# Expert results copied out of PSUM by ScalarE, low parts on VectorE alone, the residual summed by TensorE in the last norm

## The chip, the cores and the metric

The kernel runs on one core of a Trainium2 chip. Its engines are called as in the profile: PE is TensorE, ACT ScalarE, DVE VectorE, POOL GpSimd, SP SyncE; PSUM is the memory that PE writes, SBUF the one in which tiles are kept. The metric is the time of one execution on the device in microseconds (us), the median of several runs.

## What is computed

One layer of an encoder on 1024 tokens of 1024 channels (h), all in float32. A token mixer (attention, convolution, Fourier) comes first; the change doesn't touch it. Then follows the mixture of experts and the last norm:

```python
h = layer_norm(x, ln_in_g, ln_in_b)
mix = token_mixer(h, ...)
h = layer_norm(DEEPNORM_ALPHA * h + mix, ln1_g, ln1_b)
# hier_moe: 4 groups of 8 experts; each token takes the best group and the two best experts in it
for g in range(N_EXPERT_GROUPS):
    a = einsum('nd,edf->nef', xt, w_gate[g])       # d = 1024, f = 256
    u = einsum('nd,edf->nef', xt, w_up[g])
    hid = silu(a) * u * combine[:, g, :, None]
    out = out + einsum('nef,efd->nd', hid, w_down[g])
h = layer_norm(DEEPNORM_ALPHA * h + out, ln2_g, ln2_b)
```

## The kernel before

The tokens of each expert are gathered into a block of up to 128 rows; there are 33 blocks, the 32 experts (b = 0 to 31) and one for rows that overflow an expert's 128. All 33 are unrolled in one loop (L1341). Float32 products are made of three matmuls on parts rounded to another format (`mm3`, L161 to L163): high by high, high by low, low by high. So each operand is split into a high part, a copy with rounding, and a low part, the difference.

A block's weights are six tiles of 128x1024 (512 KB each): four of gate and up (g0 to g3), two of down (dL, dH). SP loads them (`fetch`, L1212) into a ring of 22 raw tiles, in the order of the list `units`; `load_next` issues the next one, and it waits until the raw tile that it overwrites has been split. For each block

- POOL gathers the rows from h in DRAM (`gather`, L1215), three blocks ahead; PE transposes them (`xtr`, L1277), ACT and DVE split them (L1280, L1283);
- ACT makes the high part of each weight tile (`high`, L1251), DVE the low part (`low`, L1255), but for g1, whose low part POOL makes in two halves of 128x512, each with a dependency written by hand (`with_start_of`) that places it beside a certain DVE low part;
- PE runs the gate and up products (`gu`), ACT the silu (L1287), DVE `hidden` (L1291), PE transposes (`htr`, L1297), ACT and DVE split the result (`hT`, L1302, L1303), and PE runs the down products (`dn`);
- DVE combines (L1315): the gathered rows times a kept scale z per row, plus `dn` from PSUM, written over the gathered rows. POOL scatters that tile (L1318) to y in DRAM, which has two rows for a token, one of each of its experts. The residual alpha·h goes into y in this way.

The work of neighbouring blocks is interleaved as the loop is written: in one turn stand the low parts and down weights of block b-1, the gate and up products of b, and the splits of b+1. Every engine's order is the order in which the code issues, in this part on SP and POOL too. One step of the overflow's bookkeeping (L1133 to L1195) is issued on DVE in each turn until it is finished. `GA` = 6 buffers hold gathered rows; ACT fills each with zeros once (L1242).

Then comes a loop over further overflow blocks (L1403), which this input doesn't enter; a barrier of all engines stands there. The last norm (L1433 to L1447) takes 8 tiles of 128 tokens: SP loads y0 and y1 (L1436, L1437), DVE adds them and takes the row sum (L1439), then the mean (L1440); ACT squares into PSUM with a sum (L1442) and takes the root (L1443); DVE takes the reciprocal (L1444), and centres, scales and shifts in two steps (L1445, L1446), and SP stores (L1447).

## Time and profile before

| | us |
|---|---|
| median of 3 runs | 992.27 (991.0 to 992.88) |
| profiled execution, its own time | 985.81 |
| its span | 984.0 |
| PE busy in the span | 892.0 (91%) |
| DVE busy | 739.7 (75%) |
| POOL busy | 506.5 (51%) |
| ACT busy | 478.4 (49%) |
| first and last silu of the 33 blocks, start | 616.3, 929.3 |
| last combine, start | 939.54 |
| first load of the last norm, issue | 944.26 |

So the span has three parts that matter here: what stands ahead of the first expert block (616 us, its last piece the routing of the last token tile), the blocks (some 313 us), and the last norm (some 40 us). The shares of busy time are means over all three, so each part is read by itself, in windows. The times of single instructions come from this one execution, which took some 6 us less than the timed runs.

### The profile page before, as it was taken

The page shows a single profiled execution, that of the slowest core. Times are in us where ns is not written, and L with a number is a line of the kernel's source. Part 1 is how long each engine was busy: PE and PEld are TensorE (multiplying, and loading weights), DVE is VectorE, ACT ScalarE, POOL GpSimd, SP SyncE. Part 2 cuts the span into 40 slices and gives each one's busy share as a digit, 9 for nine tenths or more (in the row PEclk, how much of TensorE's full clock was granted, in tenths as well). Part 3 has the DMA queues.
Part 4 walks back from the last instruction along what each step waited for, and adds up shares of the span by engine and source line. Part 5 has one row for each costly group of instructions (what it writes and reads, how often), then busy time and mean ns, then how long its engine had stood idle before and what let it go on. Part 6 is the DMA issues. An engine that isn't in the chain of part 4 may idle for free. (4 is left out here: it accounts for less than half of the span.)

```text
span 984.0 us, 11512 instructions
## 1 busy us (share of the span) xinstructions
PE 892.0 (91%) x4059; PEld 655.5 (67%) x4059; DVE 739.7 (75%) x869; ACT 478.4 (49%) x591; POOL 506.5 (51%) x286
## 2 busy tenths in 40 slices
PE   8899999999999999999999765999999999999910
PEld 5788688878865555565468654767878777878710
DVE  7643993665555767758745864999999999999848
ACT  6442331142035344344524151867777777777623
POOL 0299910350065756656645203467677888776300
PEclk9999999999999999999999885999999999999955
DMA  7043111236311000080033334899999999999167
GB/s 299 22 141 135 54 43 65 73 102 227 130 49 51 1 1 1 1 305 22 24 129 125 134 128 148 283 321 341 387 386 388 381 355 356 366 363 373 74 226 298
DMA packets 57659, 179.74 MB, mean 183 GB/s; under 512 B 10816, under 2 KB 12224, under 8 KB 57600
## 3 DMA queue, kind: packets, MB, share of 16 engines
q1 hardware_dynamic: 46800, 158.43, 43.9%
q0 software_dynamic: 9504, 16.80, 4.6%
q10 hardware_dynamic: 1296, 3.76, 1.1%
q8 instruction: 32, 0.52, 0.2%
q14 instruction: 27, 0.22, 0.1%
HBM read 162.70 MB, written 34.08 MB: 200 GB/s over the span
## 5 line engine op out<-in xcount | busy, mean ns | idle before, releaser
L685 POOL TENSOR_TENSOR ssum<-ssum,p 128x1024 f32<-128x1024 f32 x48 | 117.3, 2444 | 33.6 <-ACT p L679 29.1
L1255 POOL TENSOR_TENSOR g1l<-raw,g1h 128x512 fp32r<-128x512 f32 x66 | 87.5, 1327 | 77.2 <-DVE g2l L1255 28.1
L679 ACT ACTIVATE p<-sc 128x1024 f32<-128x1024 f32 x64 | 65.6, 1025 | 97.9 <-PE sc L163 80.1
L653 DVE TENSOR_REDUCE mx<-mp 128x1 f32<-128x1024 f32 x64 | 77.2, 1218 | 30.1 <-PE mp L652 29.8
L1318 POOL DMA_INDIRECT y_d<-gx,wql x32 | 84.3, 2635 | 25.4 <-DVE gx L1315 25.1
L161 PE MATMUL ip<-hh,wh 128*128 128x512 f32 (+1 forms) x224 | 89.5, 401 | 0.0
L162 PE MATMUL ip<-hl,wh 128*128 128x512 f32 (+1 forms) x224 | 88.8, 396 | 0.0
L163 PE MATMUL ip<-hh,wl 128*128 128x512 f32 (+1 forms) x224 | 88.4, 395 | 0.0
L1215 POOL DMA_INDIRECT gx<-h_d,wql x32 | 56.0, 1750 | 55.7 <-DVE wql L1024 50.6
L692 PE MATMUL pv<-p,v 128*64 128x512 f32 x256 | 68.0, 614 | 0.0
L1255 DVE TENSOR_TENSOR g0l<-raw,g0h 128x1024 fp32r<-128x1024 f32 x33 | 54.2, 1643 | 0.0
L1251 ACT ACTIVATE g1h<-raw 128x1024 fp32r<-128x1024 f32 x33 | 35.0, 1061 | 30.2 <-PE gu L163 21.4
L163 PEld LDWEIGHTS ip<-hh,wl 128*128 128x128 f32 (+1 forms) x224 | 41.2, 184 | 10.2 <-DVE wl L215 0.3
L162 PEld LDWEIGHTS ip<-hl,wh 128*128 128x128 f32 (+1 forms) x224 | 41.3, 184 | 9.8 <-issue 0.7
L161 PEld LDWEIGHTS ip<-hh,wh 128*128 128x128 f32 (+1 forms) x224 | 41.3, 184 | 9.7 <-issue 0.5
L1315 DVE SCALAR_TENSOR_TENSOR gx<-gx,wql,dn 128x1024 f32<-128x1024 f32 x32 | 40.7, 1272 | 2.9 <-PE dn L163 2.9
L1255 DVE TENSOR_TENSOR g3l<-raw,g3h 128x1024 fp32r<-128x1024 f32 x33 | 41.0, 1242 | 0.0
L1277 PE MATMUL xtr<-ident,gx 128*128 128x128 f32 x264 | 35.1, 277 | 6.4 <-DMA gx<-h_d,wql 6.4
L703 DVE RECIPROCAL rec<-rec 128x256 f32<-128x256 f32 x16 | 26.9, 1724 | 18.3 <-ACT rec L701 18.3
L1255 DVE TENSOR_TENSOR g2l<-raw,g2h 128x1024 fp32r<-128x1024 f32 x33 | 40.0, 1212 | 0.9 <-ACT g2h L1251 0.5
L1255 DVE TENSOR_TENSOR dL<-raw,dL 128x1024 fp32r<-128x1024 f32 x33 | 40.1, 1214 | 0.0
L1255 DVE TENSOR_TENSOR dH<-raw,dH 128x1024 fp32r<-128x1024 f32 x33 | 40.0, 1213 | 0.0
(391 smaller groups left out, 2553.2 us busy)
## 6 DMA issues: line engine op xcount, KB each, us to landing
raw<-wgu SPq DMA_DIRECT2D x128, 512.0 KB
raw<-wd SPq DMA_DIRECT2D x63, 512.0 KB
fy<-y_d SPq DMA_DIRECT2D x16, 512.0 KB
wr<-wt SPq DMA_DIRECT2D x13, 512.0 KB
xt<-x SPq DMA_DIRECT2D x8, 512.0 KB
ah_d<-al SPq DMA_DIRECT2D x8, 512.0 KB
aq<-ah_d SPq DMA_DIRECT2D x8, 512.0 KB
pa_d<-aq SPq DMA_DIRECT2D x8, 512.0 KB
```

The costliest lines, as they stand in the source:

```text
L161: T.matmul(out, lh, rh, start=start, stop=False)
L162: T.matmul(out, lh, rl, start=False, stop=False)
L163: T.matmul(out, ll, rh, start=False, stop=stop)
L653: V.tensor_reduce(mxs[h][:, t:t + 1], ps, AX.X, ALU.max)
L679: S.activation(p, ps, AF.Exp)
L685: G.tensor_tensor(ssums[h], ssums[h], p, ALU.add)
L692: T.matmul(pvs[h][64 * i:64 * i + 64], vv[t // 2][:, t % 2, 64 * h:64 * h + 64], p[:, half(i)], start=t == 0, stop=t == NT - 1)
L1215: G.indirect_dma_start(out=g, out_offset=None, in_=h1_d, in_offset=bass.IndirectOffsetOnAxis(ap=idx, axis=0), bounds_check=NTOK - 1, oob_i ...
L1255: return eng.tensor_tensor(l[:, cs], where[b, j][:, cs], f32(h[:, cs]), ALU.subtract)
L1277: T.transpose(ps[:, tok(k)], g[:, tok(k)], ident)
L1315: V.scalar_tensor_tensor(g, g, z, DN.pop(b), op0=ALU.mult, op1=ALU.add)
L1318: return G.indirect_dma_start(out=y_d, out_offset=bass.IndirectOffsetOnAxis(ap=idx, axis=0), in_=g, in_offset=None, bounds_check=2 * NTOK ...
```

## The change

1. **Results.** DVE's combine is gone. ACT copies `dn` from PSUM into one of two new tiles `yo` (L1322 of the new file), and POOL scatters that. The scales z are no longer computed. y now holds expert results alone, without the residual. `GA` falls from 6 to 4 gathered tiles.
2. **Low parts.** All of them are made by DVE, g1's as one of 128x1024; POOL keeps gathers and scatters alone. In DVE's order g3's low part now stands ahead of `hT`, and g1's behind those of the down weights. The list `units` is put in the order in which the tiles are now split.
3. **Residual.** Eight loads of h (512 KB each) stand behind the last weights, in raw tiles that have been used. In the last norm PE adds by float32 matmuls into PSUM (`fin`): alpha times the identity (`alid`) by h, the identity by y1, and for the tiles t = 1, 3, 5 (`PESUM`) by y0 too. For these three ACT copies `fin` to SBUF with the row sum; for the other five DVE adds y0 to `fin`. y1 is loaded before y0. The square goes to SBUF (over y1), not to PSUM. The rows of scale and shift (g2, b2) are loaded earlier, when the bookkeeping's tiles are free.

```diff
-GA = 6
+GA = 4
+PESUM = (1, 3, 5)
...
-    units, taken = [(0, j) for j in (0, 2, 1, 3)], [0]
+    units, taken = [(0, j) for j in range(3)], [0]
     for b in range(NS + 1):
+        units += [(b, 3)] if b < NS else []
         units += [(b - 1, 4), (b - 1, 5)] if b > 0 else []
-        units += [(b + 1, j) for j in (0, 2, 1, 3)] if b + 1 < NS else []
+        units += [(b + 1, j) for j in (1, 0, 2)] if b + 1 < NS else []
+    units += [(NS, t) for t in range(NT)]
...
+    alid = kept_w[:, 0:P]
+    S.activation(alid, ident, AF.Copy, scale=ALPHA)
     gx = [big("M", f"gx{i}") for i in range(GA)]
+    yo = [big("M", f"yo{i}") for i in range(2)]
...
-    def combine(b, g, z):
-        V.scalar_tensor_tensor(g, g, z, DN.pop(b), op0=ALU.mult, op1=ALU.add)
+    def combine(b):
+        S.activation(yo[0 if b == "ov" else b % 2], DN.pop(b), AF.Copy)
...
-            if b < NS:
-                with_start_of(low(b, 1, G, half(1)), prev)
-                load_next()
             if b > 1:
-                o, g = b - 2, gx[(b - 2) % GA]
-                combine(o, g, stat[o][3])
-                st = scatter(g, stat[o][1])
+                combine(b - 2)
+                st = scatter(yo[b % 2], stat[b - 2][1])
...
             if b + 1 < NS:
                 high(b + 1, 1)
+                low(b + 1, 1)
+                load_next()
                 xtrans(b + 1, gx[(b + 1) % GA])
-                with_start_of(low(b + 1, 1, G, half(0)), prev)
...
     for t in range(NT):
-        y0, y1, r = big("H", "fy0"), big("H", "fy1"), big("O", "fr")
+        y0, y1, r, ps = big("H", "fy0"), big("H", "fy1"), big("O", "fr"), acc("fin")
+        nc.sync.dma_start(y1, y_d[tok(NT + t)])
         nc.sync.dma_start(y0, y_d[tok(t)])
-        nc.sync.dma_start(y1, y_d[tok(NT + t)])
         sc = sp.tile([P, 4], F32, name="sc", bufs=4)
-        V.scalar_tensor_tensor(r, y0, 1.0, y1, op0=ALU.mult, op1=ALU.add, accum_out=sc[:, 0:1])
+        terms = [(alid, where[NS, t]), (ident, y1)] + ([(ident, y0)] if t in PESUM else [])
+        for n, (m, v) in enumerate(terms):
+            for i in range(2):
+                T.matmul(ps[:, half(i)], m, v[:, half(i)], start=n == 0, stop=n == len(terms) - 1)
+        if t in PESUM:
+            S.activation(r, ps, AF.Copy, accum_out=sc[:, 0:1])
+        else:
+            V.scalar_tensor_tensor(r, ps, 1.0, y0, op0=ALU.mult, op1=ALU.add, accum_out=sc[:, 0:1])
         V.tensor_scalar(sc[:, 1:2], sc[:, 0:1], -1.0 / D, None, op0=ALU.mult)
-        junk = acc("junk")
-        S.activation(junk, r, AF.Square, bias=sc[:, 1:2], accum_out=sc[:, 2:3])
+        S.activation(y1, r, AF.Square, bias=sc[:, 1:2], accum_out=sc[:, 2:3])
```

Lines of the new file stand one lower from L36 on, and further off behind the deleted ones, so the orders below are matched by what they do.

**ACT ahead of the blocks, around the last token tile.** `xT` is the copy of its transposed rows that the routing's matmuls read, `rs` a root in its norm, gx the zero fills. Before:

```order
L933 ACTIVATE rs<-mv,eps 128x1
L1242 ACTIVATE gx_4024<-eps 128x1024
L1242 ACTIVATE gx_4025<-eps 128x1024
L1242 ACTIVATE gx_4026<-eps 128x1024
L1242 ACTIVATE gx_4027<-eps 128x1024
L954 ACTIVATE xT<-xtr 128x512
L1242 ACTIVATE gx_4028<-eps 128x1024
L1242 ACTIVATE gx_4029<-eps 128x1024
L1035 ACT_TABLE_LOAD
```

and now:

```order
L1243 ACTIVATE wql<-ident 128x128
L934 ACTIVATE rs<-mv,eps 128x1
L955 ACTIVATE xT<-xtr 128x512
L1249 ACTIVATE gx_4024<-eps 128x1024
L1249 ACTIVATE gx_4025<-eps 128x1024
L1249 ACTIVATE gx_4026<-eps 128x1024
L1249 ACTIVATE gx_4027<-eps 128x1024
L1032 ACT_TABLE_LOAD
```

The last `xT` stood behind four of the six zero fills; now it stands ahead of all four, and `alid` is new.

**DVE in one late block**, from the low part of g2 to the next block's. Before:

```order
L1255 TENSOR_TENSOR g2l<-raw_4011,g2h 128x1024
L1315 SCALAR_TENSOR_TENSOR gx_4029<-gx_4029,wql,dn 128x1024
L1303 TENSOR_TENSOR hT<-htr,hT 128x256
L1255 TENSOR_TENSOR g3l<-raw_4013,g3h 128x1024
L1255 TENSOR_TENSOR dL<-raw_4014,dL 128x1024
L1255 TENSOR_TENSOR dH<-raw_4015,dH 128x1024
L1283 TENSOR_TENSOR x0l<-xtr,x0h 128x1024
L1255 TENSOR_TENSOR g0l<-raw_4016,g0h 128x1024
L1291 SCALAR_TENSOR_TENSOR sh<-gu,wql,sh 128x256
L1255 TENSOR_TENSOR g2l<-raw_4017,g2h 128x1024
```

and now:

```order
L1262 TENSOR_TENSOR g2l<-raw_4005,g2h 128x1024
L1262 TENSOR_TENSOR g3l<-raw_4006,g3h 128x1024
L1310 TENSOR_TENSOR hT<-htr,hT 128x256
L1262 TENSOR_TENSOR dL<-raw_4007,dL 128x1024
L1262 TENSOR_TENSOR dH<-raw_4008,dH 128x1024
L1262 TENSOR_TENSOR g1l<-raw_4009,g1h 128x1024
L1290 TENSOR_TENSOR x1l<-xtr,x1h 128x1024
L1262 TENSOR_TENSOR g0l<-raw_4010,g0h 128x1024
L1298 SCALAR_TENSOR_TENSOR sh<-gu,wql,sh 128x256
L1262 TENSOR_TENSOR g2l<-raw_4011,g2h 128x1024
```

The combine is gone, g1's low part has come in behind dH's, and g3's stands ahead of `hT`.

**ACT in the same place**, from one silu to the next. Before:

```order
L1287 ACTIVATE sh<-gu 128x256
L1251 ACTIVATE g2h<-raw_4007 128x1024
L1251 ACTIVATE g3h<-raw_4009 128x1024
L1302 ACTIVATE hT<-htr 128x256
L1251 ACTIVATE dL<-raw_4010 128x1024
L1251 ACTIVATE dH<-raw_4011 128x1024
L1251 ACTIVATE g1h<-raw_4014 128x1024
L1280 ACTIVATE x0h<-xtr 128x1024
L1251 ACTIVATE g0h<-raw_4012 128x1024
```

and now:

```order
L1294 ACTIVATE sh<-gu 128x256
L1258 ACTIVATE g2h<-raw_4001 128x1024
L1258 ACTIVATE g3h<-raw_4002 128x1024
L1322 ACTIVATE yo_4028<-dn 128x1024
L1309 ACTIVATE hT<-htr 128x256
L1258 ACTIVATE dL<-raw_4003 128x1024
L1258 ACTIVATE dH<-raw_4004 128x1024
L1258 ACTIVATE g1h<-raw_4005 128x1024
L1287 ACTIVATE x1h<-xtr 128x1024
L1258 ACTIVATE g0h<-raw_4006 128x1024
```

The copy of `dn` into `yo` stands between g3's high part and `hT`; the rest is as it was.

**PE behind the last block**, where before it had nothing: `raw` are the tiles of h, `wql` holds `alid`, the odd and even `fy` are y1 and y0.

```order
L1443 MATMUL fin<-raw_4001,wql 128x512 x2
L1443 MATMUL fin<-raw_4002,wql 128x512 x2
L1443 MATMUL fin<-raw_4003,wql 128x512 x2
L1443 MATMUL fin<-fy_7055,ident 128x512 x2
L1443 MATMUL fin<-fy_7074,ident 128x512 x2
L1443 MATMUL fin<-fy_7073,ident 128x512 x2
L1443 MATMUL fin<-fy_7095,ident 128x512 x2
L1443 MATMUL fin<-raw_4004,wql 128x512 x2
L1443 MATMUL fin<-fy_7114,ident 128x512 x2
L1443 MATMUL fin<-fy_7113,ident 128x512 x2
L1443 MATMUL fin<-raw_4005,wql 128x512 x2
L1443 MATMUL fin<-fy_7135,ident 128x512 x2
```

The sums of h for three tiles come first, then y1 and y0 as the tiles go on; seven such lines of two matmuls follow, 19 in all.

## Rows read from the trace of the kernel before

**Rows 1.** Windows: us, busy time of each engine, granted clock, DMA share, GB/s.
```profile
720.00:740.00 20.00, 20.00 (x97) 16.12 (x96) 20.00 (x23) 15.85 (x20) 14.20 (x9) 1.00 1.02 398
860.00:880.00 20.00, 19.57 (x98) 15.79 (x97) 20.00 (x22) 15.25 (x19) 14.39 (x9) 1.00 0.98 365
900.00:920.00 20.00, 20.00 (x99) 16.53 (x98) 19.18 (x20) 16.16 (x20) 11.80 (x8) 1.00 0.71 272
```

**Rows 2.** Line L1287: count, durations in ns (min/median/max), first and last start.
```profile
L1287 ACT ACTIVATE sh<-gu x33: 384/385/387, 616.3 to 929.3; 128x256 f32<-128x256 f32 x33
```

**Rows 3.** Timeline, DVE, one late block: start, duration, instruction.
```profile
904.79 1.28 DVE L1315 SCALAR_TENSOR_TENSOR gx<-gx,wql,dn 128x1024 f32<-128x1024 f32 x1 [0.21 <-PE dn L163]
905.99 0.42 DVE L1303 TENSOR_TENSOR hT<-htr,hT 128x256 fp32r<-128x256 f32 x1
906.32 1.22 DVE L1255 TENSOR_TENSOR g3l<-raw,g3h 128x1024 fp32r<-128x1024 f32 x1
907.45 1.22 DVE L1255 TENSOR_TENSOR dL<-raw,dL 128x1024 fp32r<-128x1024 f32 x1
...
911.06 1.27 DVE L1255 TENSOR_TENSOR g0l<-raw,g0h 128x1024 fp32r<-128x1024 f32 x1
```

**Rows 4.** Timeline, DVE and POOL, a block of the slower stretch.
```profile
783.74 2.26 DVE L1255 TENSOR_TENSOR g0l<-raw,g0h 128x1024 fp32r<-128x1024 f32 x1
...
783.61 1.30 POOL L1255 TENSOR_TENSOR g1l<-raw,g1h 128x512 fp32r<-128x512 f32 x1
...
789.34 4.34 POOL L1318 DMA_INDIRECT y_d<-gx,wql  x1 [0.31 <-DVE gx L1315]
```

**Rows 5.** Timeline, ACT, late blocks; in brackets the idle time before and its releaser.
```profile
901.98 0.39 ACT L1287 ACTIVATE sh<-gu 128x256 f32<-128x256 f32 x1 [0.55 <-PE gu L163]
...
905.00 0.39 ACT L1302 ACTIVATE hT<-htr 128x256 fp32r<-128x256 f32 x1 [0.74 <-PE htr L1297]
...
907.91 1.06 ACT L1251 ACTIVATE g1h<-raw 128x1024 fp32r<-128x1024 f32 x1 [0.62 <-DMA raw<-wd]
...
911.38 0.39 ACT L1287 ACTIVATE sh<-gu 128x256 f32<-128x256 f32 x1 [0.55 <-PE gu L163]
```

**Rows 6.** SP waits in 700:780, then in 860:905: total, times, longest.
```profile
SPq L1212 <- DVE g0l L1255: 16.0, 8, 2.4
...
SPq L1212 <- DMA raw<-wgu: 21.5, 16, 2.4
```

**Rows 7.** Timeline around the last token tile (ACT, PE, DVE), then a group of the page.
```profile
581.18 3.87 ACT L1242 ACTIVATE gx<-eps 128x1024 f32<-128x1024 f32 x4
...
585.59 1.92 PE L961 MATMUL lg<-wql,xT 128*128 128x36 f32 x8 [4.20 <-ACT xT L954]
...
587.55 0.26 DVE L966 SCALAR_TENSOR_TENSOR lg<-lg,rs,base 128x36 f32<-128x36 f32 x1 [3.60 <-PE lg L961]
...
L1215 POOL DMA_INDIRECT gx<-h_d,wql x32 | 56.0, 1750 | 55.7 <-DVE wql L1024 50.6
```

**Rows 8.** Timeline of the end: last combine, first y load, first and last DVE steps.
```profile
939.54 1.28 DVE L1315 SCALAR_TENSOR_TENSOR gx<-gx,czo,dn 128x1024 f32<-128x1024 f32 x1 [3.50 <-PE dn L163]
...
944.26 0.34 SPq L1436 DMA_DIRECT2D fy<-y_d  x1
...
949.29 1.23 DVE L1439 SCALAR_TENSOR_TENSOR fr<-fy,fy 128x1024 f32<-128x1024 f32 x1 [8.47 <-DMA fy<-y_d]
...
979.10 1.29 DVE L1446 SCALAR_TENSOR_TENSOR fr<-fr,sc,b 128x1024 f32<-128x1024 f32 x1
```

**Rows 9.** Groups of the last norm, 943.6:984: busy us, mean ns.
```profile
L1442 ACT ACTIVATE junk<-fr,sc 128x1024 f32<-128x1024 f32 x8 | 8.9, 1116 | 27.5 <-DVE sc L1440 27.5
L1446 DVE SCALAR_TENSOR_TENSOR fr<-fr,sc,b 128x1024 f32<-128x1024 f32 x8 | 10.2, 1278 | 0.0
```

**Rows 10.** Timeline, PE, fp32 matmuls of 128x512 (six records), and the window after the barrier.
```profile
572.18 2.75 PE L1327 MATMUL warm<-ones 128*128 128x512 f32 x6
...
944.00:950.00 6.00, 0.00 (x0) 0.00 (x0) 0.71 (x1) 0.00 (x0) 0.00 (x0) 0.50 0.76 249
```

More of the change, by code (lines that the diff above doesn't have):

```diff
@@ L1024, in table @@
                 self.last = V.scalar_tensor_tensor(idx.rearrange("p j e -> p (j e)"), ps, EMPTY, tabs, op0=ALU.add, op1=ALU.add)
-    def keep_scale(out, ix):
-        V.tensor_tensor(out, ix[:, 1], ix[:, 0], ALU.subtract)
-        V.tensor_scalar(out, out, -ALPHA / NTOK, ALPHA, op0=ALU.mult, op1=ALU.add)
     def combine_weights():
@@ L1234, in load_next @@
             b, j = units[taken[0]]
-            fetch(where[b, j], j, source[b], eng or nc.sync)
+            if b == NS:
+                (eng or nc.sync).dma_start(where[b, j], h1_d[tok(j)])
+            else:
+                fetch(where[b, j], j, source[b], eng or nc.sync)
             taken[0] += 1
+    alid = kept_w[:, 0:P]
+    S.activation(alid, ident, AF.Copy, scale=ALPHA)
     gx = [big("M", f"gx{i}") for i in range(GA)]
+    yo = [big("M", f"yo{i}") for i in range(2)]
     for n in range(NRAW - 7):
@@ L1329, in build @@
             high(0, j)
-            if j in (0, 2):
-                prev = low(0, j)
+            if j < 3:
+                low(0, j)
         for n in range(3):
             load_next(nc.scalar)
-        low(0, 1, G, half(0))
         next(weigh)
@@ L1359, in build @@
             if 0 < b <= NS:
+                hsplit(b - 1)
                 for j in (4, 5):
                     high(b - 1, j)
-                    prev = low(b - 1, j)
+                    low(b - 1, j)
                     load_next()
@@ L1386, in build @@
                 high(b + 1, 2)
-                prev = low(b + 1, 2)
+                low(b + 1, 2)
                 load_next()
@@ L1395, in build @@
                 source[NE] = dynamic_src(ereg)
+                g2, b2 = late_rows
+                nc.sync.dma_start(g2, A["rows"][4:5].to_broadcast([P, D]))
+                nc.sync.dma_start(b2, A["rows"][5:6].to_broadcast([P, D]))
             if b < NS:
@@ L1398, in build @@
     assert spill is None and taken[0] == len(units)
-    g2, b2 = big("L", "g2"), big("L", "b2")
-    nc.sync.dma_start(g2, A["rows"][4:5].to_broadcast([P, D]))
-    nc.sync.dma_start(b2, A["rows"][5:6].to_broadcast([P, D]))
     n_ov = nc.values_load(nov[0:1, 0:1], min_val=0, max_val=NOV)
@@ L1407, in build @@
             fetch(where["ov", j], j, dynamic_src(e), nc.sync)
[L1408 removed]
+        ci, cf = sp.tile([P, 2], I32, name="ci"), sp.tile([P, 1], F32, name="cf")
         for j in range(2):
             V.tensor_copy(ci[:, j:j + 1], idxo[:, j, bass.ds(i, 1)])
[L1411 to L1412 removed]
+        V.tensor_copy(cf, cwo[:, bass.ds(i, 1)])
         gather(gx[0], ci[:, 0:1])
@@ L1421, in build @@
         silu("ov")
-        hidden("ov", cf[:, 0:1])
+        hidden("ov", cf)
         htrans("ov")
@@ L1429, in build @@
                 emm(ps[:, half(i2)], (hT[:, 0:256], hT[:, 256:512]), part(0, 4 + k), tok(k), half(i2), k == 0, k == 1)
-        combine("ov", gx[0], cf[:, 1:2])
-        scatter(gx[0], ci[:, 1:2])
+        combine("ov")
+        scatter(yo[0], ci[:, 1:2])
     for t in range(NT):
-        y0, y1, r = big("H", "fy0"), big("H", "fy1"), big("O", "fr")
+        y0, y1, r, ps = big("H", "fy0"), big("H", "fy1"), big("O", "fr"), acc("fin")
+        nc.sync.dma_start(y1, y_d[tok(NT + t)])
         nc.sync.dma_start(y0, y_d[tok(t)])
-        nc.sync.dma_start(y1, y_d[tok(NT + t)])
         sc = sp.tile([P, 4], F32, name="sc", bufs=4)
-        V.scalar_tensor_tensor(r, y0, 1.0, y1, op0=ALU.mult, op1=ALU.add, accum_out=sc[:, 0:1])
+        terms = [(alid, where[NS, t]), (ident, y1)] + ([(ident, y0)] if t in PESUM else [])
[4 more added lines that the diff above has]
+            S.activation(r, ps, AF.Copy, accum_out=sc[:, 0:1])
+        else:
+            V.scalar_tensor_tensor(r, ps, 1.0, y0, op0=ALU.mult, op1=ALU.add, accum_out=sc[:, 0:1])
         V.tensor_scalar(sc[:, 1:2], sc[:, 0:1], -1.0 / D, None, op0=ALU.mult)
-        junk = acc("junk")
-        S.activation(junk, r, AF.Square, bias=sc[:, 1:2], accum_out=sc[:, 2:3])
+        S.activation(y1, r, AF.Square, bias=sc[:, 1:2], accum_out=sc[:, 2:3])
         S.activation(sc[:, 3:4], sc[:, 2:3], AF.Sqrt, bias=eps[:, 0:1], scale=1.0 / D)
```

20 lines of the change are left out of this document (8 added, 12 removed).

## The prediction

> **What bounds the kernel now.** I read the windows first, then single engines inside a block, then the two ends. The 33 silu instructions start from 616.3 to 929.3 [rows 2]: 32 intervals in 313.0 us, 9.78 each. Near the end one interval takes 9.40 (901.98 to 911.38), and there ACT's idle time ends on PE at both silus' side and at `hT` [rows 5]; PE is busy 20.00 of 20 us in that window while DVE has 0.8 to spare [rows 1]. So 9.40 is what PE needs for a block, and 32 x 9.40 = 300.8 would be the loop at PE's pace. The other 12.2 us are lost elsewhere. Where? In the window from 720 on DVE is busy 20.00 of 20 [rows 1]: it has no slack at all, so whatever stretches an instruction of it stretches the block. And something does: g0's low part takes 1.27 in a late block [rows 3] and 2.26 at 783.74, where POOL's half of g1's low part begins at 783.61 and runs beside it [rows 4]. That POOL instruction stands behind a scatter of 4.34 [rows 4], which is why it comes at that moment; g0's low part takes over 2 us in nine blocks. SP, up to there, waits for DVE's low parts to free raw tiles, and only later for loads to land [rows 6]. So in the blocks DVE, with POOL's collisions, is the bound, and PE is close behind it.
>
> Two more pieces count. Ahead of the blocks POOL waits for the index table (50.6 us in all, the first gather) [rows 7], and in the routing that leads to it ACT does four zero fills from 581.18 for 3.87 us before it copies the last `xT`; PE idles 4.20 for that copy and DVE 3.60 for PE [rows 7]. At the end, from the first y load (944.26) to the end of DVE's last step (979.10 + 1.29 = 980.39), 36.1 us pass, and DVE sets that pace once the first pair has landed at 949.29 [rows 8].
>
> **The change, part by part.** I take each against the profiled span of 984.0.
>
> *The start.* `xT` no longer stands behind the zero fills. PE's rows have been ready since 581.4 (585.59 less 4.20), DVE's since 583.95 (587.55 less 3.60) [rows 7]. With `xT` at 581.4, 0.57 or so long, and the eight small matmuls at 1.92 at most [rows 7], the logits are there at about 583.9, when DVE is. That brings 3.6 us, and the chain to the gathers moves as a whole. The fills now stand behind, before the table load of the combine weights; they may hold that side chain up by about 1 us, which no gather waits for. Bounds: 0 (if something else, such as the transposes at the clock PE then has, were late next) to 3.6. I take 3.6, since both idle times end on this one copy.
>
> *The blocks.* DVE loses the combine (1.20 from start to start) and gains g1's low part, 1.13 by the spacing of g3 and dL [rows 3]: by itself nearly nothing. What counts is that POOL does no subtraction any more, so no collision is left: g0's low part goes from up to 2.26 back to about 1.2 [rows 3, 4]. Seven low parts at 1.13, `hT` at 0.33 (905.99 to 906.32) and 0.4 for `hidden` (estimate from its size and `hT`) make 8.65 per block, against PE's 9.40. The overflow's steps (up to 1 us in some early blocks, estimate) fit in the difference. So DVE stops being the bound, and PE becomes it: 12.2 us gained if every interval falls to 9.40. What remains of the old loss is at least 0; the ends of this term are -4 (only the nine blocks lose their collision of about 1.0, and half of that comes back as other waits) and -14 (the first and last interval lack a part and could be below 9.40). I take -12.2.
>
> *What hides the copy on ACT.* It is about as long as g1's high part, 1.06 [rows 5], some 0.95 from start to start. `dn` ends when the combine starts, 904.79 [rows 3]; `hT` began at 905.00 after 0.74 of idle [rows 5]. So the copy fills 0.2 of that idle and pushes `hT`, dL and dH back by 0.7. Behind them stood 0.62 of idle before g1's high part, and 0.55 before the next silu [rows 5]: the push of 0.7 is taken up by these two, 1.17. PE takes `hT` and the down weights only behind the next silu, about 5 us later. In DVE's queue g1's low part then waits for its high part, and `hidden`, behind it, comes some 0.2 later than now, with about 0.8 in hand before PE transposes. Cost: 0 by this reading; it is the thinnest margin of the change, and a rival below. `yo` has two tiles, so the copy waits for a scatter of two blocks earlier, 18.8 us against 4.34 [rows 4]: free. Four gathered tiles for gathers three ahead: free too, since a tile is read by `xtr` a block before it is refilled.
>
> *The end of the last block.* ACT's copy stands in for DVE's 1.28 [rows 8], but `hT` waits behind an earlier copy, 0.7: +0.4.
>
> *The loads of h.* Eight tiles of 0.52 MB behind the last weights: 4.2 MB, 11.5 us at the 365 GB/s of rows 1. In the window from 900 the rate falls to 272 [rows 1], so the last weights are in at about 915, 25 us before the last combine. This idle time of the queue hides them; without it PE's sums would start up to 11 us late.
>
> *The last norm.* DVE is freed of three of eight additions, 3 x 1.23 [rows 8], but now every addition waits for PE, and PE has 38 float32 matmuls of 128x512. Each is two records; six records take 2.75, so one is 0.43 behind the other [rows 10], and a matmul is 0.86. 38 x 0.86 = 32.7 us. PE has been idle since 939.5, and the granted clock from 944 to 950 is 0.50 [rows 10], the lower of the two levels: the first matmuls take twice as long. I add 2.6, three matmuls' worth (ends 0 and 32.7, if the clock never rose). PE starts with h, at about the time of the first y load, 944.2, and ends at 979.5. The y tiles don't hold it: 0.52 MB take 1.3 to 1.6 us at the rates of rows 1, a pair of matmuls 1.72. Behind PE's end comes the last tile's chain: DVE's addition 1.28, the square 1.12, root and two DVE steps of which one lies beside the square, 1.28 [rows 9], some 4.7 with the small ones, and in DVE's queue the steps of tiles 5 and 6 stand between, so I take 7.4 (ends 5 and 8.5). DVE ends at 986.9 instead of 980.4: +6.5. In short, a stage of 36 us that DVE set gets a new bound of 35 us on PE plus a tail that nothing covers. That is a loss, whatever DVE saves.
>
> Sum: -3.6 - 12.2 + 0.4 + 6.5 = -8.9. On the profiled execution that is 985.8 - 8.9 = 976.9; on the median of 992.27 it is **983.4**. The timed runs are 6.5 us longer than the profiled one, and I can't say where. If it is in the blocks (more of them with the collision), it goes too, and the time is 977.
>
> **Rivals.**
>
> *The clock is up, or the norm's chain is shorter.* If PE's clock rises at once and the last chain takes 5, the norm costs +1.5 instead of +6.5: 978. For it: only a guess at how the clock rises. Against: 32.7 us on PE stand in any case.
>
> *ACT becomes the pace: slower than before.* All its margin is 0.62 + 0.55 per block [rows 5]. If the idle before g1's high part can't be used, because that instruction waits for PE or for a load in any case (as at 907.91 [rows 5]), and a copy beside PE's writes is longer than I take, each block grows by the 0.95 of the copy less the 0.55 before the silu, 0.4. Times 32 that is 12.8 us: 983.4 + 12.8 = 996, slower. From 8.9 / 32 = 0.28 us per block on the change is a loss. Against: ACT was busy 16.2 of 20 us [rows 1], and becomes 18.
>
> *The DMA becomes the pace.* A block moves 398 GB/s x 9.41 us = 3.74 MB (window from 720 [rows 1]). From 860 on SP waits for landings [rows 6] at 365 GB/s [rows 1]: 10.25 us for a block, 0.85 too much, 27 us over 32 blocks, against the 25 us by which loads now lead. Then 2 us are lost: 985.5. The same kernel moved 398 when it was asked for it, so I give this a small chance.
>
> The Trainium skill, "DMA: Bandwidth & Descriptors", section "Where 436 GB/s comes from", says that for transfers between HBM and SBUF the limit is about 358 GB/s for a core. By an estimate from that figure a block would take 10.45 us, 33.6 us too much in all, 8.6 after the lead, and the change would come out at 992, no change. The trace does not agree: 398 GB/s over 20 us from 720 [rows 1], so I hold this to 0.05.
>
> *The start brings nothing* (the next wait is as late): 987.
>
> **How the numbers follow.** (A difference of 0.2%, 2 us, is about what can be told from none here.) The forecast as summed, 0.50, 980 to 987. The extra 6.5 us goes too, 0.14, 977. Norm cheaper, 0.10, 978. Start without gain or DMA at 365, 0.07, 985 to 988. DMA by the page, or half of the loop's gain missing, 0.08, 989 to 993. ACT as the pace, 0.11, 994 to 999. Faster: the first four, 0.81, less a share of their tails and a bit of the fifth, 0.79. Same 0.08, slower 0.13. The range leaves out the ACT case and, below, both gains at once (971): 973 to 993.
>
> **What would show it.** Right: silus 9.4 apart all through, DVE with 0.5 to 1 us idle per block, no DVE low part above 1.3; POOL's index wait 3.6 shorter; PE busy without a gap for some 35 us behind the barrier, and the last DVE step about 43 us behind it. Wrong: ACT without idle ahead of the silus and pitches of 9.7 or more; SP waiting on landings while PE waits for high parts; or PE's sums over by 970, with DVE still the pace of the norm.

## The result, and the profile after

The changed kernel takes 979.95 us (median of 5 runs, 976.72 to 983.55), the kernel before 992.27: ratio 0.9885 (95% interval 0.9855 to 0.9914). It is faster by 1.2%, clear of the noise. The prediction said 983.4, and named 973 to 993.

The profiled execution took 976.72, with a span of 974.9 against the 984.0 of before. Where the 9.1 us of the spans come from, read off the two traces:

| stretch | before | after | difference | forecast |
|---|---|---|---|---|
| start to the logits of token tile 5 (of 0 to 7) | 565.47 | 567.16 | +1.7 | not touched |
| to the logits of the last token tile, 7 | 22.08 | 18.77 | -3.3 | -3.6 |
| to the first silu | 28.76 | 28.62 | -0.1 | 0 |
| 32 intervals between the silus | 312.98 | 299.73 | -13.3 | -12.2 |
| last silu to the first load of the last norm | 14.97 | 14.79 | -0.2 | +0.4 |
| from there to VectorE's last step | 36.13 | 42.24 | +6.1 | +6.5 |
| the last store | 3.61 | 3.59 | 0.0 | 0 |

The first row of the table is code that the change doesn't touch; the prediction hadn't thought of a difference there. Nearly all of it arises around 36.1 to 39.5, where PE's granted clock is at its lower level (0.50, 1.2 GHz) in the changed kernel's execution and at its upper one (1.00, 2.4 GHz) in that of before (the windows of after and then before; the last three numbers are granted clock, DMA share and GB/s):

```profile
36.10:39.50 3.40, 3.40 (x14) 2.70 (x13) 1.55 (x3) 1.39 (x2) 0.39 (x1) 0.50 0.00 0
...
36.10:39.50 3.40, 3.40 (x21) 2.79 (x20) 1.93 (x4) 2.27 (x3) 1.02 (x1) 1.00 0.00 0
```

From 30 to 36 PE is busy for 3.44 us in both. Among the traces below the clock falls at this place in some (fills_late, lows_only) and not in others (before_again, last_down), whatever the kernel, so these 1.7 us belong to the execution and not to the change. Without them the change's rows make -10.8. The rows of the change follow the forecast within 1.1 us each.

The blocks. The first line is a wait of PE from 640 to 900 before (total us, times, longest). The windows are those of [rows 1] where they exist, and the first 10 us of the last norm (us, busy time of PE, PEld, DVE, ACT, POOL, granted clock, DMA share, GB/s):

```profile
PE htr L1297 <- DVE sh L1291: 5.9, 13, 0.8
...
720.00:740.00 20.00, 20.00 (x98) 16.47 (x97) 19.69 (x22) 17.73 (x23) 5.89 (x5) 1.00 0.99 378
860.00:880.00 20.00, 20.00 (x99) 16.46 (x98) 18.86 (x21) 17.65 (x22) 5.56 (x4) 1.00 0.97 363
929.07:938.80 9.73, 9.30 (x17) 4.13 (x18) 0.00 (x1) 0.00 (x0) 0.00 (x0) 0.76 0.89 349
```

PE is busy for 20.00 of 20 us in every window from 640 to 900. That alone doesn't make it the bound, since it was 20.00 at 720 before as well, with DVE full beside it; but now no wait of PE shows from 640 to 900, and before there were 6.3 us, nearly all on DVE (the first line, of before). DVE, which had no slack at 720, has 0.3 of 20 us there (the overflow's steps still run) and 1.1 at 860; ACT rises from 15.9 to 17.7, POOL falls from 14.2 to 5.9. The silus, to be held against [rows 2]:

```profile
L1294 ACT ACTIVATE sh<-gu x33: 374/385/385, 614.6 to 914.3; 128x256 f32<-128x256 f32 x33
```

299.7 us for 32 intervals: 9.40 or 9.43 in nearly all, 7.84 for the first and 8.51 for the last. One of 10.24, in both kernels at the same block, has the overflow's matmuls on PE. In a block, the timelines of DVE and then ACT show what was in [rows 3 to 5]:

```profile
752.32 1.22 DVE L1262 TENSOR_TENSOR g1l<-raw,g1h 128x1024 fp32r<-128x1024 f32 x1
...
754.59 1.21 DVE L1262 TENSOR_TENSOR g0l<-raw,g0h 128x1024 fp32r<-128x1024 f32 x1
...
754.40 0.39 ACT L1294 ACTIVATE sh<-gu 128x256 f32<-128x256 f32 x1 [0.63 <-PE gu L164]
...
757.20 1.03 ACT L1322 ACTIVATE yo<-dn 128x1024 f32<-128x1024 f32 x1 [0.52 <-PE dn L164]
...
763.80 0.39 ACT L1294 ACTIVATE sh<-gu 128x256 f32<-128x256 f32 x1 [0.60 <-PE gu L164]
```

No low part of DVE is longer than 1.23 any more. The copy (757.20) waits 0.52 for the down products, the silu (763.80) 0.60 for the gate products, and no instruction of ACT between them waits. So of the three idle times of [rows 5] the 0.74 has become 0.52, the 0.55 has become 0.60, and the 0.62 ahead of g1's high part is used up.

What SP waits for from 700 to 780 has changed its kind ([rows 6]: DVE before):

```profile
SPq L1211 <- DMA raw<-wgu: 43.2, 31, 2.5
SPq L1211 <- DMA raw<-wd: 17.3, 16, 1.9
```

60 of 80 us are now waits for loads to land. So the raw tiles are mostly free when SP comes to them, and the landings set SP's pace, at 363 to 378 GB/s by the windows above. That is not enough for PE's pace: by the landings in the trace a weight tile is there 23 us ahead of ACT's high part at block 8, 16 to 17 at block 16, 8 to 10 at block 24, and 0.1 to 1.4 in blocks 29 to 31. The loop ends just as this lead is used up. ACT's idle time ahead of the silus of blocks 29 and 30 is 0.00 and 0.11 instead of 0.60.

The start (DVE's logits of token tiles 5 and 7, then PE's matmuls for the last, then ACT's zero fills; against [rows 7]):

```profile
567.16 0.25 DVE L967 SCALAR_TENSOR_TENSOR lg<-lg,rs,base 128x36 f32<-128x36 f32 x1 [1.59 <-PE lg L962]
...
585.93 0.25 DVE L967 SCALAR_TENSOR_TENSOR lg<-lg,rs,base 128x36 f32<-128x36 f32 x1
...
583.79 1.08 PE L962 MATMUL lg<-wql,xT 128*128 128x36 f32 x8 [0.69 <-ACT xT L955]
...
583.64 3.88 ACT L1249 ACTIVATE gx<-eps 128x1024 f32<-128x1024 f32 x4
```

PE waits 0.69 for `xT` instead of 4.20, DVE doesn't wait for PE (the logits follow the base, which ended at 585.8), and the fills come behind.

The last norm, against [rows 8, 9]: the first load, PE's sums at their beginning and end, DVE's first addition and last step:

```profile
929.07 0.33 SPq L1437 DMA_DIRECT2D fy<-y_d  x1
...
929.50 7.54 PE L1443 MATMUL fin<-raw,wql 128*128 128x512 f32 x12 [4.72 <-issue]
936.88 7.03 PE L1443 MATMUL fin<-fy,ident 128*128 128x512 f32 x16
...
962.63 1.88 PE L1443 MATMUL fin<-fy,ident 128*128 128x512 f32 x4
...
938.80 1.22 DVE L1447 SCALAR_TENSOR_TENSOR fr<-fin,fy 128x1024 f32<-128x1024 f32 x1 [17.08 <-PE fin L1443]
...
970.03 1.28 DVE L1453 SCALAR_TENSOR_TENSOR fr<-fr,sc,rx 128x1024 f32<-128x1024 f32 x1
```

PE's first twelve records take 7.4 us to the next group, the next sixteen 6.9: the granted clock is 0.76 over this window, and then each record takes 0.43. PE ends at 964.51, 35.4 after the first load, DVE 6.8 behind it. DVE, which began 5.0 behind the first load before [rows 8], now begins 9.7 behind it, since `fin` of tile 0 has to wait for three sums of h.

### The profile page after: what moved, and what is told of

Read it like the earlier page. It is cut to its first block, busy times and chain, and to the rows that moved or that the text cites. A ratio compares the mean times of both kernels' runs of the same rounds, so it can differ in the third digit from the quotient of the medians.

```text
span 974.9 us, 11616 instructions
## 1 busy us (share of the span) xinstructions
PE 920.6 (94%) x4135; PEld 674.0 (69%) x4135; DVE 715.2 (73%) x859; ACT 507.3 (52%) x629; POOL 370.9 (38%) x220
## 4 chain that ended last, share of the span: by engine, by line
PE 84%; DVE 8%; ACT 3%; issue 2%; DMA 2%; SPq 0%; POOL 0%; POOLq 0%; ACTq 0%; DVEq 0%
PE gu L164 6%; PE gu L162 6%; PE gu L163 6%; PE pv L693 6%; PE ip L164 5%; PE ip L163 5%; PE ip L162 5%; PE sc L162 3%; PE mp L653 3%; PE xtr L1284 3%; PE dn L164 3%; PE dn L163 3%; PE dn L162 3%; PE sc L163 3%; PE sc L164 3%
## 5 line engine op out<-in xcount | busy, mean ns | idle before, releaser
L1325 POOL DMA_INDIRECT y_d<-yo,wql x32 | 42.3, 1321 | 219.0 <-ACT hT L1309 206.4
L1214 POOL DMA_INDIRECT gx<-h_d,wql x32 | 49.9, 1558 | 58.0 <-DVE wql L1025 47.3
L164 PEld LDWEIGHTS ip<-hh,wl 128*128 128x128 f32 (+1 forms) x224 | 41.4, 185 | 10.3 <-DVE wl L216 0.3
L162 PEld LDWEIGHTS ip<-hh,wh 128*128 128x128 f32 (+1 forms) x224 | 41.5, 185 | 9.7 <-issue 0.5
L1322 ACT ACTIVATE yo<-dn 128x1024 f32<-128x1024 f32 x33 | 33.9, 1027 | 22.1 <-PE dn L164 22.1
L210 ACT ACTIVATE wh<-wr 128x1024 fp32r<-128x1024 f32 (+1 forms) x14 | 14.3, 1028 | 50.9 <-PE ip L163 41.8
L1262 DVE TENSOR_TENSOR g1l<-raw,g1h 128x1024 fp32r<-128x1024 f32 x33 | 40.2, 1218 | 0.2 <-ACT g1h L1258 0.2
L1262 DVE TENSOR_TENSOR g0l<-raw,g0h 128x1024 fp32r<-128x1024 f32 x33 | 40.1, 1214 | 0.0
## 6 DMA issues: line engine op xcount, KB each, us to landing
raw<-wd SPq DMA_DIRECT2D x63, 512.0 KB, 12.6
```

Of the source, the lines that this page charges most:

```text
L162: T.matmul(out, lh, rh, start=start, stop=False)
L164: T.matmul(out, ll, rh, start=False, stop=stop)
L1214: G.indirect_dma_start(out=g, out_offset=None, in_=h1_d, in_offset=bass.IndirectOffsetOnAxis(ap=idx, axis=0), bounds_check=NTOK - 1, oob_i ...
L1262: return eng.tensor_tensor(l[:, cs], where[b, j][:, cs], f32(h[:, cs]), ALU.subtract)
L1322: S.activation(yo[0 if b == "ov" else b % 2], DN.pop(b), AF.Copy)
L1325: return G.indirect_dma_start(out=y_d, out_offset=bass.IndirectOffsetOnAxis(ap=idx, axis=0), in_=g, in_offset=None, bounds_check=2 * NTOK ...
```

## The experiments

Each kernel changes the kernel before or the changed one ("after") by a few lines. All lengths below are read from their traces in the same way as the table above.

**One part of the change alone: low parts on VectorE, combine kept.** The kernel before, with the order and the loads of the changed one in the loop:

```diff
-            if b < NS:
-                with_start_of(low(b, 1, G, half(1)), prev)
-                load_next()
...
                 high(b + 1, 1)
+                low(b + 1, 1)
+                load_next()
                 xtrans(b + 1, gx[(b + 1) % GA])
-                with_start_of(low(b + 1, 1, G, half(0)), prev)
```

> The kernel before with only the second part of the change: all low parts on VectorE, none on GpSimd; the combine stays on VectorE, the last norm is as before. Theory A (VectorE's load is the bound, and a block there is the sum of its instructions): 8.65 + 1.20 = 9.85 us per block, so the 32 intervals from the first to the last silu take about 315 us, no better than the 313.0 before. Theory B (the collisions with GpSimd alone are the loss): intervals of 9.40, about 300 us. The last xT stands ahead of the zero fills here too, so the routing of the last token tile ends some 3 us earlier under both; the last norm takes 36.1 us from its first load to VectorE's last step, as before.

Measured: ratio 1.0048 (1.0031 to 1.0066) to before, a small loss. The silus, and one late block on DVE from combine to combine:

```profile
L1288 ACT ACTIVATE sh<-gu x33: 383/385/387, 619.1 to 942.6; 128x256 f32<-128x256 f32 x33
...
917.91 1.27 DVE L1316 SCALAR_TENSOR_TENSOR gx<-gx,wql,dn 128x1024 f32<-128x1024 f32 x1
919.10 1.22 DVE L1256 TENSOR_TENSOR g3l<-raw,g3h 128x1024 fp32r<-128x1024 f32 x1
...
927.77 1.27 DVE L1316 SCALAR_TENSOR_TENSOR gx<-gx,wql,dn 128x1024 f32<-128x1024 f32 x1
```

323.5 us for 32 intervals, and 9.86 in the last blocks, where the overflow's steps are over. So the sum of DVE's instructions is the block, to the hundredth: 8.65 + 1.20. In the blocks with overflow steps it is mostly 10.1 to 10.9, which the forecast of 315 had left out. Theory B falls: no low part of DVE is longer than 1.24, and yet the loop is 10.5 us longer than before. This isn't a test of the collisions alone, since DVE also takes over 1.13 us of POOL's work per block; a kernel without collisions and without that work wasn't made.

**The other part alone: copy on ScalarE, g1's low part on GpSimd.** The changed kernel with these lines back, and the loads in the old order:

```diff
+            if b < NS:
+                with_start_of(low(b, 1, G, half(1)), prev)
+                load_next()
             if b > 1:
                 combine(b - 2)
...
                 high(b + 1, 1)
-                low(b + 1, 1)
-                load_next()
                 xtrans(b + 1, gx[(b + 1) % GA])
+                with_start_of(low(b + 1, 1, G, half(0)), prev)
```

> The changed kernel with g1's low part back on GpSimd in two halves, placed and loaded as before; ScalarE's copy and the new last norm stay. Theory A: VectorE has 7.5 us of its own per block, a collision adds about 1.0, still under TensorE's 9.40, so the 32 intervals take 300 to 301 us, as in the changed kernel (299.7). Theory B (collisions are the loss): stretches of 10 us come back, 306 us or more. Four zero fills stand ahead of the last xT here, as before, so the chain from the routing to the first silu is some 3 us longer than in the changed kernel. Last norm 42 us from its first load to VectorE's last step, as in the changed kernel.

Measured: ratio 0.9991 (0.9975 to 1.0008), no difference to before. A window of the blocks, the silus, and one instruction of ACT:

```profile
800.00:820.00 20.00, 20.00 (x99) 16.47 (x98) 17.60 (x23) 17.83 (x22) 12.11 (x9) 1.00 0.98 346
...
L1293 ACT ACTIVATE sh<-gu x33: 370/385/388, 621.3 to 925.3; 128x256 f32<-128x256 f32 x33
...
886.24 1.06 ACT L1257 ACTIVATE g1h<-raw 128x1024 fp32r<-128x1024 f32 x1 [4.75 <-DMA raw<-wgu]
```

24 of the 32 intervals are as in the changed kernel, 9.40 to 9.44, though POOL makes its halves again (it is busy for 12.1 of 20 us): DVE has 2.4 us to spare. Beside a half g0's low part takes 1.40 to 1.48, and these 0.2 us cost nothing. The long collisions of [rows 4], 2.26, don't come back in this kernel, so what one of those would cost beside slack isn't shown. The copy by itself takes DVE off the path. The interval of 13.56 is the third row: ACT waits 4.75 for a load. The loads had fallen behind, at 358 to 370 GB/s from 840 on, and here they become the bound; that makes 304.1 us instead of 299.7. The last norm takes 42.2, as expected. With the fills ahead of `xT` the logits of token tile 7 come 11.1 us behind those of tile 6 instead of 7.5. (From tile 5 it is 23.6 instead of 18.8, and 22.1 and 23.5 in the two traces of before, but 1.3 of that lie between tiles 5 and 6 and go with the granted clock: 11.2 us where it is back at 1.00 by 566, in before, after and fills_late, and 12.4 to 12.7 where that takes until 570 to 572, in all the others.) So 4.4 us and 3.5 are what the second part of the change is worth on top of the first, by single traces. Why the loads ran out here isn't tried apart. That g1's raw tile is held until POOL's second half is one reading, but from 700 to 840 SP waits 100.8 of 140 us for landings and 1.4 for POOL. The other is the old order of the list, where g1 is loaded behind g0 and g2 though ACT splits it first: at block 28 g1 has 13.9 us from issue to its high part, g0 19.2 and g2 19.9, while in the changed kernel they have 18.8, 19.4 and 20.1. So g0 and g2 are as early here as there, and g1 alone is short, which speaks for the order.

**How much room ScalarE has.**

```diff
-        S.activation(yo[0 if b == "ov" else b % 2], DN.pop(b), AF.Copy)
+        for n in range(2):
+            S.activation(yo[0 if b == "ov" else b % 2], DN[b], AF.Copy)
+        DN.pop(b)
```

> The changed kernel with every copy of dn into yo done twice, one behind the other (the result is the same): 0.95 us more on ScalarE per block. The prediction's reading of ScalarE's margin (0.62 + 0.55 of idle, of which the first copy takes 0.7): 0.48 us more per block than the margin holds, intervals of about 9.88, 315 us for 32. Rival (ScalarE has enough room, since what it waits for is late anyway): 9.40, 300 us.

Measured: intervals of 9.56 to 9.67 in the middle, 305.6 in all. From silu to silu on ACT:

```profile
768.13 0.39 ACT L1294 ACTIVATE sh<-gu 128x256 f32<-128x256 f32 x1
...
770.76 2.09 ACT L1323 ACTIVATE yo<-dn 128x1024 f32<-128x1024 f32 x2 [0.34 <-PE dn L164]
...
777.70 0.39 ACT L1294 ACTIVATE sh<-gu 128x256 f32<-128x256 f32 x1
```

Neither theory: ACT's silu no longer waits and the loop is longer, but the second copy, 1.06 from start to start, costs only 0.16 to 0.27 per block. So ACT's room in the changed kernel is about 0.8 per block, not 0.47. The prediction's rival needed 0.28 us per block beyond it to turn the change into a loss: a copy of twice the length would not have done it, though not by much. The stretch ahead of the last norm is longer too, 17.8 us instead of 14.8, with PE's clock low from 928.2 on, and the span of 985.8 is 1.5 below that of before_again, which has the same stretch at the low clock in its routing.

**The kernel before, once more.**

> The kernel before, unchanged, profiled once more. If the loss in the blocks is a state that sustains itself (a long scatter, a late subtraction on GpSimd, a stretched low part), the number of slow blocks differs from execution to execution, and the 32 intervals take anything from 305 to 323 us; if it is fixed by the program, 313 again.

```profile
L1287 ACT ACTIVATE sh<-gu x33: 384/385/387, 619.7 to 932.8; 128x256 f32<-128x256 f32 x33
```

313.0 again, interval by interval within 0.04 of the first trace: the slow stretch is fixed by the program. The span is 987.3 instead of 984.0, and all of the difference lies ahead of the first silu (619.7 against 616.3). 3.1 us of it lie between the logits of token tiles 4 and 6, where the granted clock is 0.50 from 560.0 to 570.3, against 556.6 to 563.4 in the first trace; PE idles for 5.87 us up to 560.5 and 560.7 in the two. So the difference of these two executions is in PE's clock during the routing and not in the blocks. The question that the prediction left open (do the 6.5 us of the timed runs go too?) is answered for these 3.3 us alone: this execution took 989.1, and one of 992 wasn't profiled.

**The start alone.** The kernel before, with one dependency more:

```diff
-        S.activation(gx[i], eps[:, 0:1].to_broadcast([P, D]), AF.Copy, scale=0.0)
+        z = S.activation(gx[i], eps[:, 0:1].to_broadcast([P, D]), AF.Copy, scale=0.0)
+        tc.add_manual_dep(z.ins, tk[NT - 1].xt.ins.name, ...)
```

> The kernel before with one dependency added that puts the six zero fills on ScalarE behind the last xT; nothing else. Theory (both waits end on that copy, nothing else is late): from the logits of the fifth token tile to those of the last, 22.1 to 23.6 us in the two traces of before, it takes 3.4 less; the 32 intervals stay at 313.0, the last norm at 36.1; the time falls by 3.4 us (ratio 0.9966). Rival (the order there was never the point, the gain of the changed kernel came from where VectorE's low parts stand): no difference, 22 to 23.6 us.

Measured: ratio 0.9971 (0.9954 to 0.9988). The logits on DVE and PE's matmuls:

```profile
567.45 0.26 DVE L966 SCALAR_TENSOR_TENSOR lg<-lg,rs,base 128x36 f32<-128x36 f32 x1 [1.68 <-PE lg L961]
...
586.03 0.26 DVE L966 SCALAR_TENSOR_TENSOR lg<-lg,rs,base 128x36 f32<-128x36 f32 x1
...
584.05 1.08 PE L961 MATMUL lg<-wql,xT 128*128 128x36 f32 x8 [0.69 <-ACT xT L954]
```

The "fifth" token tile of the expectation is tile 5, counted from 0. 18.6 us from the first to the second row instead of 22.1 (before_again's 23.5 has the longer stretch at the low clock); loop 312.98, last norm 36.4. The order of ACT there is the whole of the term. But 0.7 of these 3.5 us are lost again up to the first silu, 29.5 us instead of 28.8: ACT makes six fills behind `xT` here, the combine weights' step on ACT behind them comes 5.2 us after the logits instead of 4.2, and the first gather 10.6 instead of 9.6. In the changed kernel, with four fills, it is 4.2 and 9.6. The prediction had said that no gather waits for such a delay.

**TensorE kept busy ahead of its sums.**

```diff
                 down(b - 1)
+            if b == NS:
+                ps = sm("warm")
+                for n in range(5):
+                    T.matmul(ps, ones, ones[:, 0:1].to_broadcast([P, 512]), start=True, stop=True)
```

> The changed kernel with five float32 matmuls of 128x512 on ones behind the last down products, so that TensorE doesn't idle for the 4.7 us ahead of its sums; their result isn't used. Theory (TensorE's sums set the end, and their first 2.2 us are lost to the low clock): the last norm, from its first load to VectorE's last step, takes 40.0 us instead of 42.2. Rival (VectorE's queue sets the end): 42.2.

The first load of the last norm, then PE:

```profile
931.82 0.33 SPq L1441 DMA_DIRECT2D fy<-y_d  x1
...
933.43 5.42 PE L1447 MATMUL fin<-raw,wql 128*128 128x512 f32 x12 [1.97 <-issue]
...
964.44 1.88 PE L1447 MATMUL fin<-fy,ident 128*128 128x512 f32 x4
```

Between the theories. The first twelve records now take 5.3 instead of 7.4 us, so the low clock did cost 2.1. But PE starts 1.6 behind the first load instead of 0.4, and ends 34.5 behind it instead of 35.4; the last norm is 41.5, and the stretch ahead of it 0.4 longer. In all 0.4 of the 2.2 us are left. Why PE starts later isn't settled.

**The sum without TensorE.**

```diff
+            V.scalar_tensor_tensor(r, where[NS, t], ALPHA, y0, op0=ALU.mult, op1=ALU.add)
+            V.scalar_tensor_tensor(r, r, 1.0, y1, op0=ALU.mult, op1=ALU.add, accum_out=sc[:, 0:1])
```

> The changed kernel with the residual added on VectorE alone: two additions for each of the eight tiles (alpha h + y0, then + y1), no sums on TensorE. Prices the choice. From rows of before, 31.1 us for eight tiles with one addition, plus 8 x 1.2, from the first landing at 5.0: 45.7 us from the first load to VectorE's last step, against 42.2 of the changed kernel and 36.1 of before. If VectorE had room in that stage, it would be 42 or less.

```profile
932.91 0.33 SPq L1439 DMA_DIRECT2D fy<-y_d  x1
...
937.95 1.22 DVE L1447 SCALAR_TENSOR_TENSOR fr<-raw,fy 128x1024 f32<-128x1024 f32 x1 [13.30 <-DMA fy<-y_d]
...
976.28 1.28 DVE L1458 SCALAR_TENSOR_TENSOR fr<-fr,sc,rx 128x1024 f32<-128x1024 f32 x1
```

44.7 us from first load to last step, 1.0 less than the 45.7 of the sum. So DVE has no room there, and TensorE's sums are worth 2.4 us against this; what costs is that the residual has to be added at all in this stage, where before it came with the combine.

**Sharing the tiles between the two.** tail_warm, and `DVESUM = (0,)`, `PESUM = (3, 5)`, where tiles of DVESUM are added as in the diff above.

> The changed kernel with the five matmuls of tail_warm, tile 0 of the last norm added on VectorE alone while TensorE sums the next ones, and y0 by TensorE for tiles 3 and 5 only. TensorE has 32 matmuls, 27.5 us, VectorE 29.9 us of work from the first landing at 5.0. Theory (the last norm is the larger of the two plus the chain of the last tile): 36 to 37 us instead of 42.2, and 974.5 us in all. Rival (the order between the two queues costs it): 39 to 42.

Ratio 0.9875 (0.9845 to 0.9904) to before, which can't be told from the 0.9885 of the changed kernel. PE around the barrier and DVE's first addition of a sum by PE, and its end:

```profile
926.34 0.63 PE L165 MATMUL dn<-dH,hT 128*128 128x512 f32 x1
...
933.89 7.11 PE L1449 MATMUL fin<-raw,wql 128*128 128x512 f32 x12 [1.99 <-issue]
...
942.76 1.23 DVE L1456 SCALAR_TENSOR_TENSOR fr<-fin,fy 128x1024 f32<-128x1024 f32 x1 [2.97 <-PE fin L1449]
...
969.23 1.28 DVE L1462 SCALAR_TENSOR_TENSOR fr<-fr,sc,rx 128x1024 f32<-128x1024 f32 x1
```

38.3 us instead of 42.2: between the theory's 36 to 37 and the rival's 39 to 42. The stretch ahead of the last norm was 16.7 instead of 14.8. Here the granted clock is 0.50 from 921.3 to 928.1, so that the last down products run at 0.43 apiece to the end, and again from 934.9 to 938.3, within PE's first sums. In tail_warm, with the same code up to there, it is 0.50 from 922.5 to 925.9 alone and the stretch takes 15.2. So the five matmuls don't secure the clock, and single traces of this end differ by 1.6 us on their own. The extra matmuls were left out of the next kernels.

**The last block's down weights split early.** In the changed kernel PE runs the last down products like this:

```profile
919.38 0.49 PE L162 MATMUL dn<-dL,hT 128*128 128x512 f32 x1 [2.11 <-ACT dL L1258]
920.64 0.79 PE L163 MATMUL dn<-dL,hT 128*128 128x512 f32 x1 [0.77 <-DVE dL L1262]
...
924.39 0.40 PE L164 MATMUL dn<-dH,hT 128*128 128x512 f32 x1
```

It waits 2.1 us for the high part of dL, which stands behind the copy and `hT` on ACT, and 0.8 for the low part. dL and dH have one pair of tiles, so they can't be split while the block before is read; the tiles of g0 and g1 are free then.

```diff
     def part(b, j):
+        if b == NS - 1 and j > 3:
+            return gate_parts[j - 4]
...
                 hidden(b, stat[b][2])
+            if b == NS - 1:
+                for j in (4, 5):
+                    high(b, j)
+                    low(b, j)
+                    load_next()
```

> The changed kernel with the down weights of the last block split as soon as its silu is under way, into the tiles of g0 and g1, which are free by then; everything else as it is. In the changed kernel TensorE waits there 2.1 us for ScalarE's high part and 0.8 for VectorE's low part behind the copy into yo, and then runs its first eight matmuls at the low clock. Theory: from the last silu to the first load of the last norm it takes 11.4 to 12.4 us instead of 14.8. Rival (the copy and hT hold it anyway): 14 or more. The 32 intervals 299.7, the last norm 42.2.

```profile
920.52 0.50 PE L162 MATMUL dn<-g0h,hT 128*128 128x512 f32 x1 [1.17 <-ACT hT L1311]
...
923.19 0.40 PE L164 MATMUL dn<-g1h,hT 128*128 128x512 f32 x1
...
928.93 0.33 SPq L1444 DMA_DIRECT2D fy<-y_d  x1
```

12.6 us from the last silu (916.4) to the first load instead of 14.8: 2.2 less, just short of the range. The last norm is 42.9, 0.7 more, since PE's clock is low for 6.1 us of it instead of 4.7. The loop takes 300.4: ACT waits 3.7 us in all for late loads in the last blocks.

**Both together.** last_down with `DVESUM = (0, 1)` and `PESUM = (3, 5)`, and the same with `PESUM = (2, 4, 6)`:

> last_down, and in the last norm tiles 0 and 1 added on VectorE alone, y0 by TensorE for tiles 3 and 5: 28 matmuls, 24.1 us and 2.2 for the clock, on TensorE; 31.1 us on VectorE from the first landing at 5.0. Theory (the larger of the two sets it): the last norm 36 to 38 us instead of 42.2; from the last silu to its first load 11.4 to 12.4; 8 us less than the changed kernel in all, 972. Rival (the queues wait for each other): 39 or more, 975.

> As best_a, with y0 by TensorE for tiles 2, 4 and 6: 30 matmuls, 25.8 us and 2.2, on TensorE; 29.9 us on VectorE from 5.0. Theory: the last norm 35.5 to 37; 971.5 in all. If VectorE isn't what sets it in best_a, this is no faster than best_a.

best_a: 974.14 us, ratio 0.9850 (0.9827 to 0.9873); last norm 38.7, 11.6 from the last silu. best_b: **972.25 us, ratio 0.9823 (0.9798 to 0.9848)**, 0.6% below the changed kernel by the two ratios, each to the kernel before as timed beside it, with intervals that just don't meet. best_a, whose last norm missed its 36 to 38, can't be told from either by time; in the traces best_b's last norm is 1.7 us shorter, within its forecast of 35.5 to 37. Its last norm in one window, PE's first sums, DVE's first addition and last step:

```profile
929.55:966.60 37.05, 27.98 (x60) 11.79 (x60) 29.68 (x44) 16.80 (x31) 0.00 (x0) 0.93 0.83 326
...
930.05 7.11 PE L1452 MATMUL fin<-raw,wql 128*128 128x512 f32 x12 [4.84 <-issue]
939.13 5.42 PE L1452 MATMUL fin<-fy,ident 128*128 128x512 f32 x12 [1.97 <-DMA fy<-y_d]
...
934.60 1.23 DVE L1454 SCALAR_TENSOR_TENSOR fr<-raw,fy 128x1024 f32<-128x1024 f32 x1 [12.05 <-DMA fy<-y_d]
...
965.28 1.28 DVE L1465 SCALAR_TENSOR_TENSOR fr<-fr,sc,rx 128x1024 f32<-128x1024 f32 x1
```

DVE is busy for 29.7 of 37.05 us, from 5.05 on; PE for 28.0, and at 939.13 it waits 1.97 for a load of y. The last norm is nearly as short as before, 37.0 against 36.1, with the residual in it.

## Why the prediction was right

**The start.** Predicted -3.6 by the two idle times of [rows 7]; -3.3 in the trace, and fills_late shows -3.5 with nothing else changed. The 0.3 are DVE, whose own chain ends at 585.8. POOL's wait for the index table fell from 50.6 to 47.3.

**The blocks.** -12.2 predicted, -13.3 measured. The size is right, as is the new bound (PE, 9.40). The first and the last interval, which the sum had at 9.40, take 7.84 and 8.51, 2.45 us less; 1.4 us are lost in others, most of them in the one of 10.24. The overflow's steps fit in DVE's margin, as said, but barely: DVE is busy for 19.97 of 20 us from 660 to 680, and has 0.15 us per block at 720 and 0.5 at 860, less than the 0.5 to 1 that was named as a sign. The prediction also took "busy 20.00 of 20" as the mark of the bound for PE and for DVE, where both had it [rows 1]; what decides is who waits. And the step that gave the reason was wrong in part: "by itself nearly nothing. What counts is that POOL does no subtraction any more". lows_only takes the collisions away and loses 10.5 us in the loop; pool_g1l lets POOL subtract and has 9.40 nearly throughout. What counts is that 1.20 us per block leave DVE for ACT. The collisions of [rows 4] came where DVE had no slack, and with slack only stretches of 0.2 us are left of them. Giving g1's low part to DVE spends most of that slack again. What came with it is that g1 is loaded in time, and the order at the start, which nobody wrote.

**The copy on ACT.** Cost 0, as predicted. The margin was sized at 0.62 + 0.55 - 0.7 = 0.47; extra_copy shows about 0.8. The push of 0.7 was right (`hT` begins 3.72 behind the silu instead of 3.02), and it eats the 0.62; but g1's high part then begins 5.88 behind the silu, a little earlier than the 5.93 of before, and 0.60 is left ahead of the next silu. The rest came out of the copy's own wait, which fell from 0.52 to 0.34 or 0.42.

**The loads.** The loads of h are hidden, as predicted: the last of them lands at 924.0, and PE's first sum of h starts 0.43 behind the first load of the last norm. The rival that the DMA becomes the pace did not cost anything to speak of in the changed kernel (ACT waits 0.3 us in all for a load in the blocks), but that is luck. Its mechanism was at work as written, 0.85 us too much per block against a lead of 25: the lead falls by about 1 us per block and is gone by block 29 of 32. In pool_g1l ACT waited 4.75 for one late load, and the loop lost 4.4. The chance was put low because the kernel before had moved 398 GB/s in one window; the rate here was 343 to 393 in windows of 20 us from 640 to 900, 370 on the mean. The Trainium skill ("DMA: Bandwidth & Descriptors", section "Where 436 GB/s comes from") gives about 358 GB/s as the limit of transfers between HBM and SBUF. The trace doesn't agree: from 700 to 720 it was 393.

**The last norm.** +6.5 predicted, +6.1 measured; PE's 32.7 and 2.6 us became 35.0, and the last chain 6.8 instead of 7.4. The sums are over at 964.5, which looks like the sign of being wrong ("over by 970"); that time was on the scale of before, and counted from the first load they end at 35.4, against 35.3 in the sum. The copy at the end of the blocks was to cost 0.4 and the stretch got 0.2 shorter, why isn't shown; PE's waits there for the last down weights are worth 2.2, as last_down shows.

**The runs.** On the profiled executions the forecast of the difference was -8.9 and the traces show -9.1. That this is so close is luck: the change's own rows make -10.8, and 1.7 us of clock at the start, which have nothing to do with it, lie the other way. The medians differ by 12.3. What the other 3 us are isn't shown: each profiled run lies below its median by a different amount (6.5 and 3.2 us), before_again puts such differences into the clock ahead of the blocks, and both profiled executions have the shorter stretch at the low clock in the routing. Beside the later experiments the kernel before took 989.0 to 989.5 (medians, on three chips); the changed kernel wasn't timed there.

## What to carry to other kernels

Where an engine is full, ask first which instruction can leave it, and only then what stretches its instructions: on an engine with slack the stretches that were left, 0.2 us each, cost nothing. A full share of busy time doesn't name the bound where two engines have it; the waits do. Look at how a lead of loads shrinks, too: here it lasted for this number of blocks and hardly for one more. Price work that is put into a last stage at that stage's own bound, plus the chain behind its last piece; a sum of 33 us on an idle engine was a loss of 6 here, until it was shared with the engine that waited for it. And look at the order that a planner makes in places that nobody meant to change: a third of the profiled gain came from there.
